# Retention by running sums of weighted keys times values, in place of products of all pairs of tiles

## The chip, the cores and the metric

One Trainium2 chip, one of its cores. The metric is the device time of one launch in microseconds (us). The core's engines are named as in the profile: PE is TensorE (matrix multiplies and transposes), DVE is VectorE, ACT is ScalarE, POOL is GpSimd, SP is SyncE, which only issues transfers here. Each engine works through its own list of instructions in the order in which the program wrote them, and waits at an instruction until what that instruction reads is there.

## The reference, cut to what matters

The reference is a two-layer transformer on 512 image tokens and 256 context tokens, 1024 wide. Each layer is a mixer (projections of the normed tokens; then windowed attention, global attention and retention; then a gated merge) and a mixture-of-experts part. The change is in retention: 4 heads, keys of 128, values of 256, with a decay per head for each of two directions. For the image tokens, after the context states `s_f` and `s_b` have been summed up:

```
def step(state, qkv):                        # one chunk of 128 tokens
    s = einsum('bihd,bjhd->bhij', qc, kc) * decay_in
    o = einsum('bhij,bjhe->bihe', s, vc) + einsum('bihd,bhde->bihe', qc * q_decay, state)
    state = chunk_decay * state + einsum('bjhd,bjhe->bhde', kc * k_decay, vc)
...
o_f = retention_chunkwise(qr, kr, vr, lg_f, s_f, False)
o_b = retention_chunkwise(qr[:, ::-1], kr[:, ::-1], vr[:, ::-1], lg_b, s_b, True)[:, ::-1]
o_ret = retention_output(o_f + o_b, u_r)
```

In layer 0 the context tokens have a retention of their own (all pairs of context tiles); in layer 1 they have none. Everything is float32.

## The kernel before

A product of two float32 matrices is made of three fp32r matmuls: each operand is split into a high part (a cast on ACT) and a low part (a subtraction on DVE), and `mm3` multiplies high by high, high by low and low by high. `split` writes the two parts one after the other, ACT first, and DVE's subtraction reads what ACT has cast.

In each layer's mixer, `dense_gen` writes the projections: 18 blocks of columns (`AK`, `A0`, ..., `R0` to `R3` for retention, `U`, and the gates `Ga`, `Gs`, `Gr`), each for 6 token tiles of 128 (4 for some blocks in layer 1), each tile 24 matmuls of 512 columns. After every 3 of these matmuls it yields the nanoseconds they are reckoned at (650), and `drive` adds them up. When the sum passes a quantum, one step of the "side" work is written in between: a step of the attention generators, and after them a step of retention, `ret_gen`. The quantum is what is left of the projections divided by the weighted number of side steps left (`left`, `weight`), so that side work and projections end together. The side work is thus cut into steps, and between two steps of retention PE gets 6 or 9 matmuls of the projections. What a step asks of ACT and DVE has that much PE time to be done, since the next step's matmuls stand in PE's list right behind.

Retention of one head, before: a table `ds` of decays over all distances (GpSimd counts, DVE multiplies, ACT takes exponentials, two pieces of 704 columns); then three turns, each for a pair of token tiles (tiles 0 to 3 are image, 4 and 5 context): four loaded blocks of q and k are transposed on PE into the PSUM tile `rqkt`, and `split` makes high and low parts of q, k and of the values (`qT`, `kT`, `VH`, `VL`). Then, for each of the 6 key tiles, a score tile against all 4 query tiles (`rst`, 3 matmuls of 512 columns), a multiplication by decays (`rt`), a split (`rpH`, `rpL`), and one step later 12 matmuls of 256 columns into the output `ro`. In layer 0 the two context tiles follow, in the same manner with 256 columns. `finish` norms the output and stores it while the next head begins.

The buffers are rings: `hp` holds 13 tiles of 512 columns (loaded q, k, v, the split scores, and what the projections store), PSUM's `oac` holds two tiles (`rqkt`, `rst`).

Of the kernel before, what the change touches and what calls it, by code (L numbers as in the profile page):

```python
# [8 lines left out]
F32 = mybir.dt.float32  # L9
# [143 lines left out]
def tile_dit(ctx, tc, a, out):  # L153
# [451 lines left out]
    def mixer(l):  # L605
# [566 lines left out]
        def ret_gen():  # L1172
# [40 lines left out]
            fins = []  # L1213
            yield from need(*[("R0", m) for m in range(6)])
            ld(0, 0)
            ld(0, 1)
            for h in range(4):
                blk = f"R{h}"

                ds = kv.tile([128, 1408], F32, tag="kv", name=f"rds{l}{h}")  # L1220
                di = pp.tile([128, 704], F32, tag="P", name="rdi")
                d2 = pp.tile([128, 704], F32, tag="P", name="rd2")
                for i in range(2):
                    sl = ds[:, i * 704:(i + 1) * 704]
                    nc.gpsimd.iota(di, pattern=[[1, 704]], base=-640 + i * 704, channel_multiplier=-1,
                                   allow_small_or_imprecise_dtypes=True)
                    nc.vector.tensor_scalar(d2, di, 0.0, lg[:, h:h + 1], op0=OP.max, op1=OP.mult)
                    nc.vector.tensor_scalar(di, di, 0.0, nlgb[:, 4 + h:5 + h], op0=OP.min, op1=OP.mult)
                    nc.vector.tensor_tensor(d2, di, d2, op=OP.add)
                    nc.scalar.activation(sl, d2, AF.Exp)  # L1230
                    yield 100
# [4 lines left out]
                for m in range(0, 6, 2):  # L1236
                    has_q = m < NIMG or ctx_q
                    if m + 2 < 6:
                        ld(h, m + 2)
                        ld(h, m + 3)  # L1240
                    ps = oac_tile("rqkt")
                    pv = ps.rearrange("p (m c t) -> p m c t", m=2, c=2)
                    vs = []
                    for i in range(2):
                        t = tl.pop((h, m + i))
                        if has_q:
                            nc.tensor.transpose(pv[:, i, 0, :], t[:, 0:128], ident)
                        nc.tensor.transpose(pv[:, i, 1, :], t[:, 128:256], ident)
                        vs.append(t[:, 256:512])
                    c = slice(m * 128, (m + 2) * 128)  # L1250
                    for j, T in ((0, qT), (1, kT)):
                        if j == 0 and not has_q:
                            continue
                        split(T[:, 0, c].rearrange("p (m t) -> p m t", m=2),
                              T[:, 1, c].rearrange("p (m t) -> p m t", m=2), pv[:, :, j, :])
# [3 lines left out]
                dctx = ot.tile([128, 2, 512], F32, tag="ot", name="rdctx")  # L1259
                for lt in range(2):  # L1260
                    cf = 256 - 128 * lt + 640
                    cb = -512 - 128 * lt + 640
                    nc.gpsimd.tensor_tensor(dctx[:, lt, :], ds[:, cf:cf + 512], ds[:, cb:cb + 512], op=OP.add)
                for grp in range(2 if ctx_q else 1):
                    qts = list(range(NIMG)) if grp == 0 else [4, 5]
                    nt = len(qts)
                    w = nt * 128
                    q0 = qts[0] * 128
                    kts = list(range(6)) if grp == 0 else [4, 5]
# [3 lines left out]
                    for ki, kt in enumerate(kts + [None]):  # L1273
                        if (grp == 1 or not ctx_q) and h < 3 and ki == max(len(kts) - RLD, 0):
                            yield from need(*[(f"R{h + 1}", m) for m in range(6)])
                            ld(h + 1, 0)
                            ld(h + 1, 1)
                        nxt = None
                        if kt is not None:
                            ps = oac_tile("rst")  # L1280
                            ks = slice(kt * 128, (kt + 1) * 128)
                            mm3(ps[:, 0:w], kT[:, 0, ks], kT[:, 1, ks], qT[:, 0, q0:q0 + w], qT[:, 1, q0:q0 + w],
                                True, True)
                            if grp == 0 and kt >= NIMG:
                                dd = dctx[:, kt - 4, :]
                            else:
                                c = 640 - 128 * (kt - qts[0])
                                dd = ds[:, c:c + w]
                            t = half("rt")
                            nc.vector.scalar_tensor_tensor(t[:, 0:w], ps[:, 0:w], ksc, dd, op0=OP.mult, op1=OP.mult)  # L1290
                            ph = half("rpH", F32R)
                            pl = half("rpL", F32R)
                            split(ph[:, 0:w], pl[:, 0:w], t[:, 0:w])
                            nxt = (ki, kt, ph, pl)
# [1145 lines left out]
```

## Time and profile before

| | us |
|---|---|
| time, median of 3 runs (lowest to highest) | 2956.02 (2948.24 to 2957.04) |
| the profiled execution: its own time | 2947.53 |
| its span, from the first to the last instruction | 2945.7 |
| PE busy in the span | 2778.4 (94%) |
| DVE busy | 1808.9 (61%) |
| ACT busy | 1281.2 (43%) |
| POOL busy | 362.3 (12%) |

An engine counts as busy while it has an instruction at work; matmuls are pipelined, so the time that a matmul costs is read from the start of one to the start of the next and not from its duration. Retention lies at 780 to 985 us (layer 0) and 2255 to 2420 us (layer 1).

### The profile page before, as it was taken

The numbers are of one execution on the slowest core, as the hardware profiler recorded it, in microseconds if no ns is written. First come the engines' busy times: TensorE is split into PE (matmuls) and PEld (weight loads), VectorE is DVE, ScalarE is ACT, GpSimd is POOL, SyncE is SP. The second block draws the span as 40 slices with busy tenths as digits, with TensorE's granted clock in tenths as the row PEclk, the third lists the DMA queues.
The fourth block names the chain that finished last, engine by engine and source line by source line (L and its number), as shares of the span: only waits on it lengthen the run. The fifth ranks groups of instructions, "written<-read, shape, count | busy, mean of one in ns | idle before, by whom it ended". The sixth has DMA issues, their size and how long they took to land. (4 is left out here: it accounts for less than half of the span.)

```text
span 2945.7 us, 42092 instructions
## 1 busy us (share of the span) xinstructions
PE 2778.4 (94%) x15259; PEld 2224.0 (75%) x15259; DVE 1808.9 (61%) x3222; ACT 1281.2 (43%) x2380; POOL 362.3 (12%) x427
## 2 busy tenths in 40 slices
PE   7999999999999999988999799999999999989986
PEld 4788888888887777776777478878988887767653
DVE  5676567667555456568676576667676655667432
ACT  4444445445444212227666454444455442216332
POOL 1220000000011000013322131100000100013211
PEclk8999999999999999998999999999999999989998
DMA  6333222223243577668999832222233447688998
GB/s 243 133 110 106 90 76 81 96 70 104 95 151 130 180 258 257 257 220 295 346 363 371 292 118 91 82 88 92 73 97 123 147 147 294 214 314 329 370 371 302
DMA packets 203925, 557.89 MB, mean 189 GB/s; under 512 B 27046, under 2 KB 51750, under 8 KB 203712
## 3 DMA queue, kind: packets, MB, share of 16 engines
q1 hardware_dynamic: 175840, 502.85, 47.6%
q0 software_dynamic: 10752, 25.03, 3.4%
q10 hardware_dynamic: 17120, 27.27, 2.5%
q8 instruction: 121, 1.98, 0.3%
q14 instruction: 92, 0.75, 0.1%
HBM read 462.22 MB, written 96.77 MB: 190 GB/s over the span
## 5 line engine op out<-in xcount | busy, mean ns | idle before, releaser
L114 DVE TENSOR_TENSOR wl<-raw,wh 128x1024 fp32r<-128x1024 f32 x474 | 565.2, 1220 | 148.9 <-ACT wh L102 144.6
L102 ACT CAST wh<-raw 128x1024 fp32r<-128x1024 f32 x474 | 484.7, 1050 | 351.9 <-DMA raw<-oT 131.4
L903 ACT ACTIVATE P<-sc,st 128x768 f32<-128x768 f32 (+4 forms) x240 | 176.2, 734 | 339.4 <-DVE st L901 211.0
L901 DVE TENSOR_REDUCE st<-sc 128x1 f32<-128x768 f32 (+4 forms) x240 | 178.5, 744 | 119.0 <-PE sc L179 113.3
L937 ACT CAST ptH<-pt 128x512 fp32r<-128x512 f32 x264 | 142.9, 591 | 125.1 <-PE pt L922 104.7
L179 PE MATMUL psb<-wl,wh 128*128 128x512 f32 x480 | 188.7, 393 | 7.1 <-DVE wl L114 7.1
L179 PE MATMUL psb<-wh,wh 128*128 128x512 f32 x480 | 191.7, 399 | 0.0
L179 PE MATMUL psb<-wh,wl 128*128 128x512 f32 x480 | 188.0, 392 | 2.2 <-DVE wl L114 2.2
L947 DVE TENSOR_TENSOR ptL<-pt,ptH 128x512 fp32r<-128x512 f32 x264 | 169.4, 681 | 9.2 <-ACT ptH L937 7.0
L922 PE MATMUL pt<-ident,P 128*128 128x128 f32 x1056 | 141.4, 275 | 13.8 <-ACT P L903 11.1
L922 PEld LDWEIGHTS pt<-ident,P 128*128 128x128 f32 x1056 | 119.7, 140 | 44.5 <-ACT P L903 30.2
L179 PE MATMUL psR<-wh,hH 128*128 128x512 f32 (+1 forms) x384 | 150.8, 393 | 0.0
L179 PE MATMUL psR<-wl,hH 128*128 128x512 f32 (+1 forms) x384 | 146.8, 382 | 2.7 <-DVE wl L114 2.7
L179 PE MATMUL psR<-wh,hL 128*128 128x512 f32 (+1 forms) x384 | 147.2, 383 | 0.0
L909 DVE TENSOR_SCALAR P<-P,st 128x768 f32<-128x768 f32 (+3 forms) x240 | 130.0, 542 | 8.5
L179 PEld LDWEIGHTS psb<-wh,wh 128*128 128x128 f32 x480 | 90.3, 188 | 45.3 <-issue 20.1
L495 POOL TENSOR_SCALAR rstd<-ss 128x4 f32<-128x4 f32 (+2 forms) x70 | 22.8, 326 | 825.8 <-ACT h L501 355.3
L179 PEld LDWEIGHTS psb<-wl,wh 128*128 128x128 f32 x480 | 90.5, 189 | 28.3 <-DVE wl L114 10.9
L179 PE MATMUL sc<-swkT,swqs 128*128 128x256 f32 x704 | 109.2, 281 | 2.2 <-ACT P L903 2.2
L179 PEld LDWEIGHTS psb<-wh,wl 128*128 128x128 f32 x480 | 90.5, 189 | 22.5 <-DVE wl L114 3.5
L179 PE MATMUL yps<-wh,hidT 128*128 128x512 f32 x320 | 105.6, 400 | 1.5 <-ACT wh L102 1.5
L1110 DVE COPY sc<-sink 128x1 f32<-128x1 f32 x160 | 25.7, 160 | 130.2 <-PE sc L179 123.1
(511 smaller groups left out, 6905.7 us busy)
## 6 DMA issues: line engine op xcount, KB each, us to landing
raw<-in_w_in_dram SPq DMA_DIRECT2D x136, 512.0 KB
raw<-in_w_gate_dram SPq DMA_DIRECT2D x128, 512.0 KB
raw<-in_w_up_dram SPq DMA_DIRECT2D x128, 512.0 KB
raw<-in_w_down_dram SPq DMA_DIRECT2D x128, 512.0 KB
raw<-in_w_mod_dram SPq DMA_DIRECT2D x96, 512.0 KB
raw<-in_w_br_dram SPq DMA_DIRECT2D x48, 512.0 KB
raw<-oT SPq DMA_DIRECT2D x30, 512.0 KB
raw<-in_w_out_dram SPq DMA_DIRECT2D x16, 512.0 KB
```

The lines of the kernel that those rows point to most:

```text
L102: self.nc.scalar.copy(c.h, c.raw)
L114: self.nc.vector.tensor_tensor(c.l, c.raw, c.h.bitcast(F32), op=OP.subtract)
L179: nc.tensor.matmul(ps, lhs, rhs, start=start, stop=stop, skip_group_check=share)
L495: nc.gpsimd.tensor_scalar(r[:, 0:cnt], ss, four / n, four * EPS, op0=OP.mult, op1=OP.add)
L901: nc.vector.reduce_max(st[:, 1, h:h + 1], s[:, 0:self.ns], axis=AX.X, negate=True)
L903: nc.scalar.activation(self.P[h][:, 0:self.ns], s[:, 0:self.ns], AF.Exp, bias=st[:, 1, h:h + 1], accum_out=st[:, 2, h:h + 1])
L909: nc.vector.tensor_scalar(self.P[h][:, 0:self.nk], self.P[h][:, 0:self.nk], st[:, 3, h:h + 1], None, op0=OP.mult)
L922: nc.tensor.transpose(pt[:, c * 256 + h * 128:c * 256 + (h + 1) * 128], self.P[2 * x + h][:, i * 128:(i + 1) * 128], ident)
L937: nc.scalar.copy(ph, src)
L947: nc.vector.tensor_tensor(pl, src, ph.bitcast(F32), op=OP.subtract)
L1110: nc.vector.tensor_copy(s[:, nk:nk + 1], sink[:, hd:hd + 1])
```

## The change

Retention of the image tokens no longer multiplies every key tile by every query tile. Four states, each a 128x256 matrix for either direction side by side (512 columns), are built one after the other: `state(0)` sums weighted context keys times values, `state(i)` multiplies the one before by a decay and adds the products of one key tile for each direction. `apply(i)` multiplies weighted queries by a state into the output. Scores are left only for each tile with itself (12 matmuls of 128 columns). The turns, now `turned(m)`, besides make the weighted queries (`rq`, split into `rQH`, `rQL`) and, from the loaded keys, keys weighted for both directions (`rk`, split into `rKH`, `rKL`). The context pair is turned first; in layer 1 it needs no transposes. The table of decays becomes 384 columns, two rows of 128 for the queries and six columns for the keys. A head has 12 steps in layer 0 (15 before) and 9 in layer 1 (12 before).

```diff
-                for m in range(0, 6, 2):
...
-                        nc.tensor.transpose(pv[:, i, 1, :], t[:, 128:256], ident)
...
-                    for i in range(2):
-                        split(VH[:, m + i, :], VL[:, m + i, :], vs[i])
-                    yield 300
...
-                    for ki, kt in enumerate(kts + [None]):
...
-                            mm3(ps[:, 0:w], kT[:, 0, ks], kT[:, 1, ks], qT[:, 0, q0:q0 + w], qT[:, 1, q0:q0 + w],
-                                True, True)
...
+                def turned(m):
...
+                        for j, T in ((0, qT), (1, kT)):
+                            split(T[:, 0, c].rearrange("p (m t) -> p m t", m=2),
+                                  T[:, 1, c].rearrange("p (m t) -> p m t", m=2), pv[:, :, j, :])
+                    if m < NIMG:
+                        q = half("rq")
+                        for x in range(2):
+                            nc.vector.scalar_tensor_tensor(
+                                q[:, x * 256:(x + 1) * 256].rearrange("p (m t) -> p m t", m=2), pv[:, :, 0, :], ksc,
+                                rw[:, x, :][:, None, :].to_broadcast([128, 2, 128]), op0=OP.mult, op1=OP.mult)
+                        QL[m] = half("rQL", F32R)
+                        split(QH[:, m // 2, :], QL[m], q)
+                    k = half("rk")
                     for i in range(2):
...
+                        for x in range(2):
+                            w = 3 * x + (m + i == (5 if x else 4))
+                            o = (2 * i + x) * 128
+                            nc.vector.tensor_scalar(k[:, o:o + 128], ts[i][:, 128:256], wk[:, w:w + 1], None,
+                                                    op0=OP.mult)
+                    KH[m], KL[m] = half("rKH", F32R), half("rKL", F32R)
+                    split(KH[m], KL[m], k)
                     for i in range(2):
...
+                        split(VH[:, m + i, :], VL[:, m + i, :], ts[i][:, 256:512])
+
+                def state(i):
+
+                    ps = oac_tile("rup")
+                    for x in range(2):
+                        kts = (4, 5) if i == 0 else (4 - i,) if x else (i - 1,)
+                        for kt in kts:
+                            m, j = kt - kt % 2, kt % 2
+                            ks = slice((2 * j + x) * 128, (2 * j + x + 1) * 128)
+                            for n, (k_, v_) in enumerate(((KH, VH), (KH, VL), (KL, VH))):
+                                mm(ps[:, x * 256:(x + 1) * 256], k_[m][:, ks], v_[:, kt, :],
+                                   kt == kts[0] and n == 0, kt == kts[-1] and n == 2, share=True)
...
+                    if i == 0:
+                        nc.scalar.copy(S[0][:, 0:512], ps)
+                    for x in range(2 if i else 0):
+                        c = slice(x * 256, (x + 1) * 256)
+                        nc.vector.scalar_tensor_tensor(S[0][:, c], old[:, c], wk[:, 3 * x + 2:3 * x + 3], ps[:, c],
+                                                       op0=OP.mult, op1=OP.add)
+                    split(S[1][:, 0:512], S[2][:, 0:512], S[0][:, 0:512])
+                    return S[1], S[2]
+
+                def apply(i, sh, sl):
+
+                    for x, t in ((0, i), (1, 3 - i)):
...
+                        for n, (q_, s_) in enumerate(((qh, sh), (qh, sl), (ql, sh))):
+                            mm(ov[:, t, :], q_, s_[:, c], False, i == 3 and n == 2, share=True)
...
+                fetch(h, 0)
+                turned(4)
+                yield 300
+                fetch(h, 2)
+                turned(0)
+                s0 = state(0)
+                yield 1500
+                turned(2)
+                yield 300
...
+                ph, pl = half("rpH", F32R), half("rpL", F32R)
+                split(ph, pl, t)
+                s1 = state(1)
+                yield 1500
...
+                apply(0, *s0)
+                s2 = state(2)
+                yield 1500
+                apply(1, *s1)
+                s3 = state(3)
+                yield 1500
...
+                apply(2, *s2)
+                yield 700
+                apply(3, *s3)
...
-        left = [5 * 2 * nq + 22, 5 * (4 * nq + 1), 4 * (15 if ctx_q else 12)]
+        left = [5 * 2 * nq + 22, 5 * (4 * nq + 1), 4 * (12 if ctx_q else 9)]
```

How the change moves instructions shows at three places of the first heads of layer 0. The first is PE's list where the last turn's parts are first used. Before, three score matmuls (`rst`) stand behind the projection's matmuls (`psGs`), and six more of those stand before the next three:

```order
L179 MATMUL psGs_4_8079<-wh_7858,hL_4_622 128x512
L179 MATMUL rst<-rqT_8052,rkT_8053 128x512 x3
L179 MATMUL psGs_4_8079<-wh_7858,hH_4_621 128x512
L179 MATMUL psGs_4_8079<-wl_7859,hH_4_621 128x512
L179 MATMUL psGs_4_8079<-wh_7858,hL_4_622 128x512
L179 MATMUL psGs_5_8151<-wh_7411,hH_5_689 128x512
L179 MATMUL psGs_5_8151<-wl_7412,hH_5_689 128x512
L179 MATMUL psGs_5_8151<-wh_7411,hL_5_690 128x512
L179 MATMUL rst<-rqT_8052,rkT_8053 128x512 x3
```

After, the transposes of `turned(2)` are followed by nine projection matmuls (the last three are shown), the 12 short scores and, with nothing in between, the six matmuls of `state(1)` (`rup`), the last three of which read the keys and values of tile 3:

```order
L179 MATMUL psGs_1_8202<-wh_8103,hH_1_406 128x512
L179 MATMUL psGs_1_8202<-wl_8104,hH_1_406 128x512
L179 MATMUL psGs_1_8202<-wh_8103,hL_1_407 128x512
L179 MATMUL rst<-rqT_8165,rkT_8166 128x128 x12
L179 MATMUL rup<-rVH_8167,rKH 128x256
L179 MATMUL rup<-rVL_8168,rKH 128x256
L179 MATMUL rup<-rVH_8167,rKL 128x256
L179 MATMUL rup<-rVH_8167,rKH 128x256
L179 MATMUL rup<-rVL_8168,rKH 128x256
L179 MATMUL rup<-rVH_8167,rKL 128x256
L179 MATMUL psGs_2_8342<-wh_7752,hH_2_475 128x512
```

So `state(1)` now stands one step behind the turn that makes what it reads. The second place is DVE's list of the same turns. Before, a turn is four subtractions (`rqT`, `rkT`, twice `rVL`), and after three turns come the scores:

```order
L188 TENSOR_TENSOR rqT_8052<-rqkt,rqT_8052 128x256
L188 TENSOR_TENSOR rkT_8053<-rqkt,rkT_8053 128x256
L188 TENSOR_TENSOR rVL_8055<-rqkv,rVH_8054 128x256 x2
L188 TENSOR_TENSOR rqT_8052<-rqkt,rqT_8052 128x256
L188 TENSOR_TENSOR rkT_8053<-rqkt,rkT_8053 128x256
L188 TENSOR_TENSOR rVL_8055<-rqkv,rVH_8054 128x256 x2
L1290 SCALAR_TENSOR_TENSOR rt<-rst,rds_8021 128x512
```

After, `turned(0)`, the split of the first state and the beginning of `turned(2)`:

```order
L188 TENSOR_TENSOR rqT_8165<-rqkt,rqT_8165 128x256
L188 TENSOR_TENSOR rkT_8166<-rqkt,rkT_8166 128x256
L1269 SCALAR_TENSOR_TENSOR rq<-rqkt,rds_8138 128x256 x2
L188 TENSOR_TENSOR rQL<-rq,rQH 128x512
L1279 TENSOR_SCALAR rk<-rqkv,rds_8138 128x128 x4
L188 TENSOR_TENSOR rKL<-rk,rKH 128x512
L188 TENSOR_TENSOR rVL_8168<-rqkv,rVH_8167 128x256 x2
L188 TENSOR_TENSOR rSL<-rS,rSH 128x512
L188 TENSOR_TENSOR rqT_8165<-rqkt,rqT_8165 128x256
L188 TENSOR_TENSOR rkT_8166<-rqkt,rkT_8166 128x256
```

The values' low parts, which `state` reads, moved from third and fourth in a turn to eleventh and twelfth, behind the weighted queries and keys. The third place is ACT's list between the two image turns of the second head: the cast of the first state, then the previous head's output (`roo`, with its store) and a cast of projection weights (`wh`), and only then the casts of the next turn:

```order
L1302 COPY rS<-rup 128x512
L187 CAST rSH<-rS 128x512
L1208 COPY roo<-rot 128x1024
L1209 DMA oT_109<-roo 128x4x256
L102 CAST wh_8686<-raw_8107 128x1024
L187 CAST rqT_8574<-rqkt 128x256
L187 CAST rkT_8575<-rqkt 128x256
L187 CAST rQH<-rq 128x512
L187 CAST rKH<-rk 128x512
```

What moved there: the state's copy and cast, and `rQH` and `rKH`, are new in ACT's list, so a turn has two more casts, each behind a result of DVE's.

## Rows read from the trace of the kernel before

**Rows 1.** The page, busy time of each engine (us, share of the span, instructions).
```profile
PE 2778.4 (94%) x15259; PEld 2224.0 (75%) x15259; DVE 1808.9 (61%) x3222; ACT 1281.2 (43%) x2380; POOL 362.3 (12%) x427
```

**Rows 2.** Busy time by stretch: us, PE, PEld, DVE, ACT, POOL, PEclk, DMA share, GB/s.
```profile
780.00:985.00 205.00, 200.16 (x1082) 170.20 (x1081) 102.50 (x178) 82.50 (x183) 24.53 (x31) 0.99 0.37 124
2255.00:2420.00 165.00, 164.48 (x892) 139.30 (x891) 95.52 (x155) 72.47 (x151) 19.77 (x23) 1.00 0.45 149
```

**Rows 3.** PE's timeline, one step of retention: start, us, what, count.
```profile
804.47 0.40 PE L179 MATMUL psGs<-wh,hH 128*128 128x512 f32 x1
...
806.54 0.84 PE L179 MATMUL rst<-rqT,rkT 128*128 128x512 f32 x3
807.22 0.28 PE L179 MATMUL ro<-rVH,rpH 128*128 128x256 f32 x1
...
808.65 0.40 PE L179 MATMUL psGs<-wh,hH 128*128 128x512 f32 x1
```

**Rows 4.** PE's timeline: a 128-column matmul of windowed attention.
```profile
605.21 0.22 PE L179 MATMUL sc<-maskr,identr 128*128 128x128 f32 x1
605.27 0.45 PE L179 MATMUL psU<-wh,hH 128*128 128x512 f32 x1
```

**Rows 5.** PE's timeline: the four transposes of a turn.
```profile
793.30 0.28 PE L1247 MATMUL rqkt<-ident,rqkv 128*128 128x128 f32 x1
...
793.66 0.47 PE L179 MATMUL psGs<-wh,hH 128*128 128x512 f32 x1
```

**Rows 6.** ACT's timeline, the same turn, and a split of scores.
```profile
793.94 0.37 ACT L187 CAST rqT<-rqkt 128x256 fp32r<-128x256 f32 x1 [0.35 <-PE rqkt L1248]
794.80 0.37 ACT L187 CAST rkT<-rqkt 128x256 fp32r<-128x256 f32 x1 [0.49 <-DVE rqT L188]
795.07 0.71 ACT L187 CAST rVH<-rqkv 128x256 fp32r<-128x256 f32 x2
...
801.77 0.62 ACT L187 CAST rpH<-rt 128x512 fp32r<-128x512 f32 x1 [1.38 <-DVE rt L1290]
```

**Rows 7.** DVE's timeline, the same turn, and the same split of scores.
```profile
794.35 0.42 DVE L188 TENSOR_TENSOR rqT<-rqkt,rqT 128x256 fp32r<-128x256 f32 x1 [1.58 <-ACT rqT L187]
795.21 0.42 DVE L188 TENSOR_TENSOR rkT<-rqkt,rkT 128x256 fp32r<-128x256 f32 x1 [0.44 <-ACT rkT L187]
...
800.16 0.75 DVE L188 TENSOR_TENSOR rVL<-rqkv,rVH 128x256 fp32r<-128x256 f32 x2
801.05 0.69 DVE L1290 SCALAR_TENSOR_TENSOR rt<-rst,rds 128x512 f32<-128x512 f32 x1
802.43 0.69 DVE L188 TENSOR_TENSOR rpL<-rt,rpH 128x512 fp32r<-128x512 f32 x1 [0.69 <-ACT rpH L187]
```

**Rows 8.** DVE's timeline: narrow operations elsewhere, and the scaling of a head's output.
```profile
169.96 1.12 DVE L801 SCALAR_TENSOR_TENSOR nA<-psA,rstd,gq 128x128 f32<-128x128 f32 x4
386.28 0.49 DVE L909 TENSOR_SCALAR P<-P,st 128x512 f32<-128x512 f32 x1
833.37 1.65 DVE L1199 SCALAR_TENSOR_TENSOR ron<-ro,rstd,rz 128x256 f32<-128x256 f32 x4
```

**Rows 9.** Costliest groups: weight splits of the projections (busy, mean ns, idle before).
```profile
L114 DVE TENSOR_TENSOR wl<-raw,wh 128x1024 fp32r<-128x1024 f32 x474 | 565.2, 1220 | 148.9 <-ACT wh L102 144.6
L102 ACT CAST wh<-raw 128x1024 fp32r<-128x1024 f32 x474 | 484.7, 1050 | 351.9 <-DMA raw<-oT 131.4
```

**Rows 10.** One tile's instructions: the stored output (count, ns min/median/max).
```profile
L1208 ACT COPY roo<-rot x12: 577/1010/1019, 841.5 to 2418.1; 128x1024 f32<-128x1024 f32 x8, 128x512 f32<-128x512 f32 x4
```

**Rows 11.** PE's timeline around its longest wait in retention.
```profile
938.25 0.33 PE L1247 MATMUL rqkt<-ident,rqkv 128*128 128x128 f32 x1 [3.42 <-DMA rqkv<-nat0R]
...
939.10 0.64 PE L179 MATMUL psGr<-wh,hH 128*128 128x512 f32 x1
...
942.10 0.63 PE L179 MATMUL psGr<-wl,hH 128*128 128x512 f32 x1
```

**Rows 12.** Busy time by stretch behind that wait (columns as in Rows 2).
```profile
940.00:942.00 2.00, 2.00 (x6) 1.61 (x5) 0.75 (x3) 1.26 (x2) 0.00 (x0) 0.50 0.19 69
```

More of the change, by code (lines that the diff above doesn't have):

```diff
@@ L1232, in ret_gen @@
+                nc.scalar.activation(strip, d2[:, 0:384], AF.Exp)
+                yield 100
                 qT = kv.tile([128, 2, 768], F32R, tag="kv", name=f"rqT{l}{h}")
@@ L1259, in ret_gen @@
[L1259 to L1269, printed above, removed]
+                QH = ot.tile([128, 2, 512], F32R, tag="ot", name="rQH")
@@ new lines, in apply, with next_head @@
+                def apply(i, sh, sl):
+                    for x, t in ((0, i), (1, 3 - i)):
+                        qs = slice(x * 256 + t % 2 * 128, x * 256 + t % 2 * 128 + 128)
+                        qh, ql = QH[:, t // 2, qs], QL[t - t % 2][:, qs]
+                        c = slice(x * 256, (x + 1) * 256)
+                        for n, (q_, s_) in enumerate(((qh, sh), (qh, sl), (ql, sh))):
+                            mm(ov[:, t, :], q_, s_[:, c], False, i == 3 and n == 2, share=True)
+                def next_head():
+                    if h < 3:
+                        yield from need(*[(f"R{h + 1}", m) for m in range(6)])
+                        fetch(h + 1, 4)
@@ new lines, in ret_gen @@
+                fetch(h, 0)
[7 more added lines that the diff above has]
+                yield 300
+                ps = oac_tile("rst")
+                for t in range(NIMG):
+                    c = slice(t * 128, (t + 1) * 128)
+                    for n, (k, q) in enumerate(((0, 0), (0, 1), (1, 0))):
+                        mm(ps[:, c], kT[:, k, c], qT[:, q, c], n == 0, n == 2, share=True)
@@ new lines, in ret_gen @@
+                yield 1500
+                o = att_tile("ro")
+                ov = o.rearrange("p (i d) -> p i d", i=4)
+                for i in range(NIMG):
+                    c = slice(i * 128, (i + 1) * 128)
+                    for n, (p_, v_) in enumerate(((ph, VH), (ph, VL), (pl, VH))):
+                        mm(ov[:, i, :], p_[:, c], v_[:, i, :], i % 2 == 0 and n == 0, False, share=True)
+                apply(0, *s0)
+                s2 = state(2)
+                yield 1500
+                apply(1, *s1)
@@ L1270, in ret_gen @@
+                s3 = state(3)
+                yield 1500
+                if not ctx_q:
+                    yield from next_head()
+                apply(2, *s2)
+                yield 700
+                apply(3, *s3)
+                fins.append(1)
+                side.append(finish(h, list(range(NIMG)), o))
+                yield 100
+                if ctx_q:
                     o = att_tile("ro")
@@ L1272, in ret_gen @@
                     pend = None
-                    for ki, kt in enumerate(kts + [None]):
[L1274 to L1277, printed above, removed]
+                    for kt in (4, 5, None):
+                        if kt == 4:
+                            yield from next_head()
                         nxt = None
@@ L1289, in ret_gen @@
-                            t = half("rt")
[L1290 to L1294, printed above, removed]
+                            c = 128 - 128 * (kt - 4)
+                            t = half("rt")
+                            nc.vector.scalar_tensor_tensor(t[:, 0:256], ps[:, 0:256], ksc, strip[:, c:c + 256],
+                                                           op0=OP.mult, op1=OP.mult)
@@ L1306, in ret_gen @@
                     fins.append(1)
-                    side.append(finish(h, qts, o))
+                    side.append(finish(h, [4, 5], o))
                     yield 100
@@ L2023 @@
 TURN = [(1, 4), (1, 5), (1, 6)]
-RLD = 2
 MCAP = 3
```

84 lines of the change are left out of this document (46 added, 38 removed).

## The prediction

> **What bounds the kernel now.** I read the page's busy times first: PE is busy for 2778.4 of 2945.7 us, no other engine for more than 61% [rows 1]. Then the stretches of retention: in layer 0 PE is busy 200.2 of 205 us, in layer 1 164.5 of 165, while DVE is busy 50 and 58% of them and ACT 40 and 44% [rows 2]. So PE sets the pace there. A matmul taken out is worth its spacing in PE's list, and every wait at a matmul is paid in full, because the projections' matmuls stand behind it in the same list. That DVE and ACT have room on average doesn't say that they have it within one step.
>
> **What PE saves.** Prices are start to start. Nine projection matmuls take 2.07 us, 0.23 each; three scores of 512 columns 0.68; twelve output matmuls of 256 columns 1.43, 0.12 each [rows 3]. A matmul of 128 columns takes 0.06 [rows 4]. Four transposes take 0.36 [rows 5]. Taken out per head: 18 scores of 512 (4.1 us) and 72 output matmuls (8.6), 12.7 us. Put in: 30 matmuls for the states, 24 that apply them and 12 within tiles, 66 of 256 columns (7.9 us), and 12 scores of 128 (0.7), 8.6 us. That is 4.1 us less in each of four heads; layer 1 also loses the two key transposes of the context pair, 4.3 us. Layer 0's context part stays. In all 34 us. Should the 128-column scores cost as much as 256 (0.12), 6 us of it would go.
>
> **What the turns cost.** Here is the other side. In a turn ACT and DVE hand the same data back and forth. From rows: ACT's cast of q to DVE's subtraction 0.41 us (793.94 to 794.35), from there to ACT's next cast 0.45, again 0.41 to DVE, then 0.34 for DVE to get on [rows 6, 7]: at 1.6 us q and k are split. Today two subtractions of values follow, 0.33 apart (0.75 for two of 0.42) [rows 7], and the turn is done in 2.3 us, about what one step gives PE to do.
>
> After the change, a turn of image tiles goes on like this, as DVE's list has it. Two weighted queries from PSUM: 0.39 each, the spacing of the four 256-column operations that took 1.65 us [rows 8]; to ACT, cast of 512 columns, back to DVE: 0.5 and 0.66 (801.77 to 802.43) [rows 6, 7]; low part 0.61: now 3.8 us. Four key products of 128 columns: at most 0.26 each (1.12 us for four of 0.34, from PSUM), at least 0.12 (a quarter of the 512-column scaling in 0.49) [rows 8]; I take 0.26, whose width is the same: 4.8. To ACT 0.1, cast 0.66, low part 0.61: 6.2. Two low parts of values: 6.9 us. The values that `state` wants come last, three times later than today.
>
> Between the two image turns DVE also has the first state's low part, which waits for ACT's copy and cast (0.6 each, as wide as `rpH` [rows 6]). With time 0 at the first cast of `turned(0)`: DVE has done that turn at 6.9, ACT the state's cast at 7.2, DVE its low part at 7.9. The second turn's first subtraction starts there, so its clock runs from 7.5: keys are split at 9.1, the values of tile 3 at 14.4.
>
> PE on the same clock, by rows 3 to 5, in a head of layer 1 with nine projection matmuls between steps: `state(0)` ends at 1.15, nine matmuls 3.2, transposes 3.6, nine matmuls 5.65, six scores 6.0. The next scores need the keys split at 9.1: a wait of 3.1 us. Then scores and the first half of `state(1)` until 9.9; its second half needs the low values of tile 3: a wait of 4.5 us, until 14.4. So **7.6 us of waits** in a head that has none now, against 4.3 saved. After that the list eases: `apply` reads states made a step earlier.
>
> In layer 0 `turned(4)` has a part in it too. Its chain (splits 1.6, keys 1.1, cast 0.66, low parts 0.61 and 0.67) takes 4.7 us, and PE reaches `state(0)` at about 2.2: with eight matmuls left behind the last value, 2 us of waits, and 9.2 in the head.
>
> Later heads have more in the way. In layer 0, ACT's list puts a weight cast (1.05 us [rows 9]) or a gate, and the output of the head before (1.0 [rows 10]), between the two turns: 2 us more; and the scaling of the last output stands ahead of `rt`, so that the next output matmuls wait some 0.7. That makes 11.9 in each of three heads. In layer 1, two heads have six projection matmuls in place of nine once (0.7 less cover), three have the 1.65 us scaling before `rt` (about 1.1 paid), and the third has two weight splits of 1.2 between the turns and one behind them: about 39 us for the four. Sum: 9.5 (with a gate in the first head) + 36 + 39 = **84 us**. From below: key products at 0.12 take off 11 us, and with nothing in later heads but the clean chain it would be 56. From above: 3.4 us more per head if a load or a buffer comes late, 111.
>
> **The clock.** The one long wait in retention today, 3.42 us for a load, was followed by matmuls 0.43 us apart in place of 0.23 for some 3 us [rows 11], with a granted clock of 0.50, which is 1.2 GHz [rows 12]: 1.6 us for eight matmuls. The new second wait is longer than that. I take 6 us in all, between 0 and 13 (eight heads at 1.6), since part of the slow time falls where PE then waits for `rpL` anyway.
>
> The Trainium skill (TensorE: Matmul & The Clock Gate, section "HAM oscillation — how this bites in real kernels") says that a loop which lets TensorE stand in each round finds its clock at half speed each time, and that this comes on top of the wait. By that rule all eight heads pay and the sum is 7 us higher. By the row alone one wait of this size did so, and this trace has no other in retention.
>
> **The rest.** The decay tables shrink on GpSimd, DVE and ACT; PE waits for none of these three there (0.5 us of idle in all of layer 1's stretch [rows 2]), and they stand a step ahead of the turn that reads them, so I count nothing; if they came late, the turn would start later by at most one such step. The loads are as many and still one step ahead. With 12 and 9 steps per head the quantum grows by 4 and 6% (weighted steps 290 to 278 and 221 to 209), so attention is spread a little wider; its matmuls and the projections' are the same, and I count nothing. `rt` and `rpL` (six times per head, now once) leave DVE with a total about 2 us larger per head; its 42 to 50% of free time hides that outside the turns.
>
> **Sum.** 84 of waits, 34 saved, 6 of clock: +56 us on the execution's own 2947.5, 1.8 us more than its span: 3003.5. That execution is 8.5 us under the median of the three runs and within their spread; I don't add the difference. About 0.3% (9 us) is what a measurement of this kernel can tell from no change.
>
> **The rivals.** First, *faster*: the turns keep up, and the 34 us remain in part. The place is DVE's list in `turned`; the point from which it decides is a wait of 4.25 us per head, that is, values of tile 3 at 11 us and not at 14.4, each turn in 5.2. For it speaks that DVE waits for ACT during a third of a turn in my chain, and that I took the dearer price for the keys. Against it, the alternation is in the lists and its rows are of this very stretch. Without any wait it would be 2913 us; I put it at 2925. Second, *about even*: only the clean chain is paid, with cheap keys, and attention gains by its wider spacing: waits of 40 to 55 us, 2953 to 2968. Third, *worse*: the ring `hp`. Queries and keys of a head now stay in 8 of its 13 buffers while projections store from the rest, so a load, or a cast on ACT, waits for a store. Each would add about what the late load cost, 3.4 us [rows 11]; in every head, with the clock, that is 111 + 13 - 34, 3038 us and more. It speaks for it that such a wait is there today, against it that only one head has it. Last, *the change doesn't do what it says*: PE isn't relieved because 128-column scores are bound by their weight loads. The row of the short matmul [rows 4] speaks against it; at 0.12 it costs 6 us and changes nothing else.
>
> **Chances.** My forecast, 2970 to 3035 us: 0.66. Faster rival 0.12; even 0.12, half of it within 0.3% of no change; worse 0.10. So faster 0.12, same 0.06, slower 0.82. The range reaches into the even rival and a little into the worse one: 2955 to 3045.
>
> **What would show it.** In the new profile PE is idle some 10 us per head where it now has next to none, with waits of `rup` and `rst` for `rVL` and `rkT` on DVE, longest about 4 us; scores start to start at 0.06; a granted clock of 0.5 behind the waits. DVE shows `rVL` of tile 3 14 us after the first cast of `turned(0)`. I am wrong if `rup` finds its operands ready, if keys cost well under 0.26 us, or if DVE and ACT overlap where I have them alternate.

## The result, and the profile after

The changed kernel takes 3019.91 us (median of 4 runs, 3015.40 to 3023.89), the kernel before 2952.61 (4 runs beside it): 1.0227 times as long, 95% interval 1.0200 to 1.0255. The profiled execution takes 3015.4 us with a span of 3013.6, 67.9 more than the span of before. So it is slower, 67 us where 56 were forecast.

The page's busy times, which answer to [rows 1]:

```profile
PE 2785.0 (92%) x15155; PEld 2228.3 (74%) x15155; DVE 1831.2 (61%) x3362; ACT 1303.5 (43%) x2440; POOL 342.0 (11%) x451
```

PE runs 104 matmuls fewer and is yet busy 6.6 us longer, and idle for 228.6 us in place of 167.3. DVE and ACT hardly have more to do. The stretches of retention, by stretch as in [rows 2] (they lie later here, and hold less projection work):

```profile
800.00:1025.00 225.00, 192.45 (x985) 160.99 (x984) 118.57 (x255) 97.99 (x219) 12.33 (x37) 0.91 0.35 119
2285.00:2480.00 195.00, 165.77 (x837) 139.20 (x836) 109.57 (x238) 86.30 (x190) 8.89 (x36) 0.86 0.36 119
```

PE, which had next to no idle time there, now stands for 32.6 of 225 us and 29.2 of 195, and its granted clock falls from 0.99 and 1.00 to 0.91 and 0.86: part of the time it stands at the lower of its two levels, 1.2 GHz in place of 2.4. What it waits for, in the waits of layer 0's stretch and then of layer 1's (waiter, releaser, us in total, times, longest):

```profile
PE rup L179 <- ACT rVH L187: 13.5, 7, 2.7
PE rst L179 <- ACT rkT L187: 9.3, 4, 3.3
PE rqkt L1262 <- DMA rqkv<-nat0R: 4.7, 1, 4.7
PE rup L179 <- DVE rVL L188: 2.3, 8, 0.4
...
PE rqkt L1262 <- DMA rqkv<-nat1R: 11.1, 4, 6.4
PE rup L179 <- ACT rVH L187: 10.4, 5, 2.7
PE rst L179 <- ACT rkT L187: 3.9, 3, 1.6
```

States (`rup`) wait for values and scores (`rst`) for keys, both products of the turns: with the smaller waits of these two kinds that are left out here, 42.4 us in both layers. Loads take 15.8 us besides. One later head of layer 0 in PE's timeline (start, us, what, count, idle time before):

```profile
867.43 0.60 PE L1262 MATMUL rqkt<-ident,rqkv 128*128 128x128 f32 x4
869.03 0.38 PE L179 MATMUL rup<-rVH,rKH 128*128 128x256 f32 x1 [1.00 <-ACT rVH L187]
869.79 0.39 PE L179 MATMUL rup<-rVL,rKH 128*128 128x256 f32 x1 [0.37 <-DVE rVL L188]
...
871.19 1.04 PE L1205 MATMUL rot<-ident,ron 128*128 128x128 f32 x8
...
875.74 0.40 PE L179 MATMUL psGr<-wh,hL 128*128 128x512 f32 x1
876.46 0.89 PE L179 MATMUL rst<-rqT,rkT 128*128 128x128 f32 x6 [0.32 <-ACT rS L1302]
880.65 1.58 PE L179 MATMUL rst<-rqT,rkT 128*128 128x128 f32 x6 [3.31 <-ACT rkT L187]
882.02 0.52 PE L179 MATMUL rup<-rVH,rKH 128*128 128x256 f32 x1
...
885.19 0.58 PE L179 MATMUL rup<-rVH,rKH 128*128 128x256 f32 x1 [2.22 <-ACT rVH L187]
885.98 0.58 PE L179 MATMUL rup<-rVL,rKH 128*128 128x256 f32 x1 [0.20 <-DVE rVL L188]
886.36 0.41 PE L179 MATMUL rup<-rVH,rKL 128*128 128x256 f32 x1
886.57 0.63 PE L179 MATMUL psGr<-wh,hH 128*128 128x512 f32 x1
...
889.83 0.39 PE L179 MATMUL psGr<-wh,hL 128*128 128x512 f32 x1
```

Read start to start, the head loses more than the idle times in brackets (7.4 us). From 875.97, when the last projection matmul is through, to 886.57 are 10.6 us, for twelve scores and six state matmuls that need 2.0: 8.6 lost. At the first state 3.4 us (867.79 to 871.19) go for 1.44 of work: 2.0 lost. Then eight `psGr` matmuls take 3.26 us (886.57 to 889.83) in place of 1.84: the granted clock is 0.50 from 879.4 to 889.6. Together 12.0 us. The same turns in DVE's timeline and in ACT's:

```profile
870.53 0.43 DVE L188 TENSOR_TENSOR rqT<-rqkt,rqT 128x256 fp32r<-128x256 f32 x1 [0.47 <-ACT rqT L187]
...
873.18 0.69 DVE L188 TENSOR_TENSOR rQL<-rq,rQH 128x512 fp32r<-128x512 f32 x1 [0.69 <-ACT rQH L187]
873.79 0.87 DVE L1279 TENSOR_SCALAR rk<-rqkv,rds 128x128 f32<-128x128 f32 x4
875.34 0.69 DVE L188 TENSOR_TENSOR rKL<-rk,rKH 128x512 fp32r<-128x512 f32 x1 [0.69 <-ACT rKH L187]
875.95 0.75 DVE L188 TENSOR_TENSOR rVL<-rqkv,rVH 128x256 fp32r<-128x256 f32 x2
877.09 0.69 DVE L188 TENSOR_TENSOR rSL<-rS,rSH 128x512 fp32r<-128x512 f32 x1 [0.38 <-ACT rSH L187]
...
885.17 0.75 DVE L188 TENSOR_TENSOR rVL<-rqkv,rVH 128x256 fp32r<-128x256 f32 x2
```

```profile
870.14 0.36 ACT L187 CAST rqT<-rqkt 128x256 fp32r<-128x256 f32 x1
...
876.96 1.01 ACT L1208 COPY roo<-rot 128x1024 f32<-128x1024 f32 x1
...
878.42 1.05 ACT L102 CAST wh<-raw 128x1024 fp32r<-128x1024 f32 x1 [0.45 <-ACT roo L1208]
879.37 0.36 ACT L187 CAST rqT<-rqkt 128x256 fp32r<-128x256 f32 x1
```

The first turn runs from 870.14 to 876.70, 6.56 us; the second starts at 879.37, behind the head's output and a weight cast; its last value is done at 885.92. ACT and DVE alternate: DVE is idle 0.69 us at each cast of 512 columns.

### The profile page after: what moved, and what is told of

Read it like the earlier page. It is cut to its first block, busy times and chain, and to the rows that moved or that the text cites. A ratio compares the mean times of both kernels' runs of the same rounds, so it can differ in the third digit from the quotient of the medians.

```text
span 3013.6 us, 42077 instructions
## 1 busy us (share of the span) xinstructions
PE 2785.0 (92%) x15155; PEld 2228.3 (74%) x15155; DVE 1831.2 (61%) x3362; ACT 1303.5 (43%) x2440; POOL 342.0 (11%) x451
## 5 line engine op out<-in xcount | busy, mean ns | idle before, releaser
L937 ACT CAST ptH<-pt 128x512 fp32r<-128x512 f32 x264 | 142.8, 591 | 137.8 <-PE pt L922 122.0
L922 PE MATMUL pt<-ident,P 128*128 128x128 f32 x1056 | 142.8, 276 | 18.6 <-ACT P L903 12.9
L179 PEld LDWEIGHTS psb<-wl,wh 128*128 128x128 f32 x480 | 90.8, 189 | 28.6 <-DVE wl L114 11.1
```

Source lines behind the costliest of these rows:

```text
L179: nc.tensor.matmul(ps, lhs, rhs, start=start, stop=stop, skip_group_check=share)
L922: nc.tensor.transpose(pt[:, c * 256 + h * 128:c * 256 + (h + 1) * 128], self.P[2 * x + h][:, i * 128:(i + 1) * 128], ident)
L937: nc.scalar.copy(ph, src)
```

## The experiments

Times are medians; each kernel ran beside the kernel before, and the ratio is to that. "Cover" is the PE work that stands in PE's list between a turn and the first matmul that needs it.

**More steps between the turns.** `yield 300` or `yield 1500` lets PE do one more step of projections.

```
                 turned(4)
                 yield 300
+                yield 300
...
                 s0 = state(0)
                 yield 1500
+                yield 1500
                 turned(2)
                 yield 300
+                yield 300
+                yield 300
...
-        left = [..., 4 * (12 if ctx_q else 9)]
+        left = [..., 4 * (16 if ctx_q else 13)]
```

> Four more steps per head (one behind the turn of tiles 4 and 5, one behind the first state, two behind the turn of tiles 2 and 3), and the planner's count of steps raised to 16 and 13. Each step gives PE some 2 us of projection work. Theory (a turn is a chain of ACT and DVE that is longer than its cover): of the 42 us that PE waits for turns under 10 are left, matmuls of 512 columns at half clock in retention fall from 75 to under 15, and the time is 2925 to 2955 us; the loads' 16 us may stay. Rival A (the 34 us of saved matmuls are not there): the waits go but the time stays at 2960 to 2985. Rival B (loads and buffers hold PE up, the turn only shows it): the waits change their names and the time stays over 2990.

2983.95 us, ratio 1.0107 (1.0090 to 1.0124): 36 us off the change, but 29 above the theory's range and inside that of rival A. The turns' waits did go (42.4 us in the change, 1.5 here, all in layer 0). But others remain: PE waits 10.5 us for `ron`, the scaled output, and 15.6 for loads, and 45 matmuls of 512 columns still run at half clock, where I had asked for under 15. Rival A is right in a small part: the scores, now without a wait, show their price, in PE's timeline and in that of the weight loads:

```profile
859.86 1.45 PE L179 MATMUL rst<-rqT,rkT 128*128 128x128 f32 x12
861.14 0.34 PE L179 MATMUL rup<-rVH,rKH 128*128 128x256 f32 x1
```

```profile
859.63 1.53 PEld L179 LDWEIGHTS rst<-rqT,rkT 128*128 128x128 f32 x12
861.08 0.19 PEld L179 LDWEIGHTS rup<-rVH,rKH 128*128 128x128 f32 x1
```

Twelve scores take 1.28 us, 0.107 each, and not the 0.06 of [rows 4]. Their weight loads (PEld, twelve in 1.45 us) keep the same pace: taken singly, scores and loads both start 0.11 us apart. So the change saves 3.5 us per head in layer 0 and not 4.1, 29 in all.

**Two steps only**, both behind `turned(2)`, and 14 and 11 in `left`.

> Two more steps per head, both behind the turn of tiles 2 and 3, ahead of the scores; the planner counts 14 and 11. Theory: 4 us more cover at the place of the two longest waits: the scores' wait for keys goes and that for the last values falls to under 1 us per head; the waits at the first state (some 1.4 us per head) and for loads stay. 2970 to 2988 us, above the kernel with four more steps by 20 to 45. Rival B: 3000 us or more.

3008.29 us, 1.0190 (1.0173 to 1.0207): 20 above the theory's range, and inside the rival's. The longest waits of layer 1's stretch, then DVE's timeline in layer 0 where its like stands:

```profile
PE rot L1205 <- DVE ron L1199: 21.1, 3, 7.4
PE psGs L179 <- DVE wl L114: 7.0, 2, 4.3
```

```profile
908.59 0.43 DVE L188 TENSOR_TENSOR rqT<-rqkt,rqT 128x256 fp32r<-128x256 f32 x1 [1.04 <-ACT rqT L187]
...
914.00 0.75 DVE L188 TENSOR_TENSOR rVL<-rqkv,rVH 128x256 fp32r<-128x256 f32 x2
914.67 0.87 DVE L1199 SCALAR_TENSOR_TENSOR ron<-ro,rstd,rz 128x256 f32<-128x256 f32 x2
```

`finish` counts its pauses in steps, while turns take time. With two steps put in, the transposes of the head before come up while DVE is still in the second turn, and `ron` stands behind all of it. The waits for keys are gone, and those for values are down from 27.4 to 8.6 us; but 41 us of waits for `ron` over both layers took their place.

**Weighted queries left out**: no `rq`, `rQH`, `rQL`; `apply` reads `qT`.

```
-                        qh, ql = QH[:, t // 2, qs], QL[t - t % 2][:, qs]
+                        qh, ql = qT[:, 0, qs], qT[:, 1, qs]
```

> The weighted queries are left out: no products of queries by their tables, no cast and no low part of them; the states are applied to the unweighted high and low parts of the queries, so that the output lacks that weighting. PE's list stays as it is. Theory: by the durations after the change (0.75 for the two products, 0.62 the cast, 0.6 the low part, and the handoffs) each turn of image tiles is some 2.1 us shorter, the second one ends 4.2 us earlier, and of the waits for keys and values 20 to 30 us go, with part of the slow clock: 2980 to 2998 us. Rival B (loads and buffers): 3005 us or more.

3041.51 us, 1.0303 (1.0285 to 1.0322), slower than the change. But it leaves out part of the result, so that other tokens go to other experts, and layer 0's expert stage runs matmuls that the other kernels don't have (one tile's instructions in that stage):

```profile
L179 PE MATMUL g<-w,xH x16: 390/564/797, 1686.6 to 1696.9; 128*128 128x512 f32 x16
```

Between the same two matmuls at its ends that stage takes 442 us, and 382 in the change. So I read it by stretch: up to the end of retention layer 0 is 19 us shorter than the change (995.9 against 1015.2), and layer 1, from its first projection to its output projection, 17 us (775.1 against 792.0). These 36 us lie in the 22 to 40 that the theory's range asked for, and the waits for keys and values fall from 42.4 to 18.7 us while those for loads stay. The whole time says nothing of it.

**Loads one step earlier.**

```
             fetch(0, 4)
+            fetch(0, 0)
...
                         fetch(h + 1, 4)
+                        fetch(h + 1, 0)
...
-                fetch(h, 0)
+                fetch(h, 2)
                 turned(4)
                 yield 300
-                fetch(h, 2)
                 turned(0)
```

> The loads of tiles 0 and 1 of the next head are issued with those of tiles 4 and 5, and tiles 2 and 3 a step earlier too: two more buffers of the ring are held. Theory: only the 15.8 us that PE waits for loads can go, with some slow clock behind them: 2998 to 3010 us, and the waits for keys and values stay at 38 to 48 us. Rival B: without late loads the turns start earlier and keep up, 2985 us or less. If the ring of buffers is too small for it, DVE or ACT waits for buffers and it is 3015 us or more.

3016.46 us, 1.0223 (1.0206 to 1.0240), not to be told from the change, and above the theory's range. PE's waits for loads fall in layer 1 from 11.1 to 2.0 us, but 4.0 for a weight (0.6 in the change) and 2.3 more for values come in their place. In the change those loads come late because SP issues them in order behind weight loads that wait for a buffer (SP's timeline of the change, layer 1):

```profile
2355.05 5.28 SPq L83 DMA_DIRECT2D raw<-in_w_in_dram  x2
2360.38 2.11 SPq L1180 DMA_DIRECT2D rqkv<-nat1R  x4
```

**The turns' work alone, in the kernel before**: the products, casts and low parts of keys are made in each turn, those of queries in the two image turns, and no matmul reads them; all matmuls stay, no states.

```
                     for j, T in ((0, qT), (1, kT)):
...
+                    if m < NIMG:
+                        q = half("rq")
...
+                        split(half("rQH", F32R), half("rQL", F32R), q)
+                    k = half("rk")
...
+                    split(half("rKH", F32R), half("rKL", F32R), k)
```

> The kernel before, all its matmuls, with the work of the new turns alone added to its turns: two products of queries, four of keys, their casts and low parts, whose results nothing reads. No states and no strip of decay; loads as before. Theory (the turn's chain is longer than a step): PE now waits at the first scores for the second turn's queries and keys, 2 to 5 us in each of eight heads and more where a weight cast or an output stands between: 2970 to 2995 us. Rival (ACT and DVE have the room, the loss comes from what PE reads in the changed kernel or from its loads): 2950 to 2962 us.

3033.20 us, 1.0286 (1.0267 to 1.0306): 81 us more, where the theory had 18 to 43: beyond its range, and far from the rival's. Waits of layer 0's stretch:

```profile
PE rst L179 <- DVE rq L1260: 14.2, 4, 5.3
PE rot L1205 <- DVE ron L1199: 9.4, 3, 3.6
```

The scores read no `rq`. Their wait is for the PSUM tile: `oac` holds two, and DVE reads `rq` out of the second turn's `rqkt` before a score may be written there. So this wait is not at the place where the change has its own, but it is for the same thing, the progress of ACT and DVE in the turns. Loads don't explain it: PE waits 3.8 us for them in both layers, 3.6 in the kernel before. So the loss is there without a state, with the old matmuls, and comes from what the turns put on ACT and DVE.

**Transposes of the output two steps later**, on top of the four steps: `pause(4)` in place of `pause(2)` in `finish`.

> The kernel with four more steps per head, and the transposes of a head's scaled output two steps later (five steps in place of three stay as they are, the second pause is four in place of two). With the four steps the waits for turns had gone, and the transposes waited 10.5 us for the scaled output on DVE in their place. Theory (turn work fills DVE, so that what stands behind it in DVE's list comes late): these waits go with what they cost around them, 2966 to 2976 us, the loads' 16 us stay. Rival (PE finds another wait, since DVE or ACT is the bound of this stretch): 2980 us or more.

2975.09 us, 1.0089 (1.0071 to 1.0107), as the theory said: no wait for `ron` is left in retention, and those for loads stay at 15.2 us.

**Loads earlier too**, as above and for the first head a step ahead.

> As the kernel with four more steps and later transposes, and the loads of a head's tiles one step earlier, the first head's a step ahead of its turn. Theory: the waits of PE for loads fall from 16 to under 4 us and no other wait takes their place, now that the turns have cover: 2945 to 2960 us. Of 29 us saved in matmuls (the 128-column scores cost 0.107 us each, not 0.06) no more than a third is then seen, the rest is lost to slow clock, restarts and the attention stretch of layer 1. Rival (the earlier loads only move the wait to weights, as they did alone): 2965 us or more.

2980.66 us, 1.0106 (1.0089 to 1.0123): missed, and in the rival's range. In retention PE waits for loads for 1.6 us in place of 15.2, and layer 1's retention is 7 us shorter. But other waits do take their place: those of the states for values grow from 8.7 to 14.0 us, and 44 matmuls of 512 columns run at half clock in place of 25. The attention ahead of layer 1's retention is 7.5 us longer too (618.2 and 610.7), with waits of `pt` for the softmax's `P` of 16.9 us in place of 9.6. The profiled execution (2972.93 us) is the shortest of the four and as long as that of the kernel without this edit (2973.61), so the trace doesn't show the 6 us that the medians differ by.

**Keys on GpSimd and one more step**: `nc.gpsimd.tensor_scalar` for `k`, `yield 1500` ahead of `ro`, 17 and 14 steps.

> As the kernel before it in this set, with the products of keys on GpSimd in place of DVE and one more step ahead of the output matmuls. Theory (DVE's list in a turn sets the end): each turn is some 0.8 us shorter on DVE and the waits for rpH go: 2938 to 2955 us, if GpSimd takes under 0.6 us for a product of 128 columns. Rival: GpSimd is slower than that, or slows DVE while both run, and the keys come late at the states: 2960 us or more.

2959.69 us, 1.0035 (1.0022 to 1.0048), 5 above the theory's range. The costliest group of GpSimd:

```profile
L1281 POOL TENSOR_SCALAR rk<-rqkv,rds 128x128 f32<-128x128 f32 x96 | 71.2, 759 | 63.2 <-DMA rqkv<-nat0R 28.8 <-ACT rds L1239 26.7 <-PE rup L179 6.5
```

A product of keys takes 0.76 us on average (0.60 in the median, at most 1.69), longer than the theory asked, and waits of the states for values stay at 12.5 us. Still it is 21 us less than without the two edits; which of them gave it isn't shown.

**Values first, queries last, and two steps out again** (those behind `state(0)` and one behind `turned(2)`; 15 and 12, as many as before the change). Keys stay on GpSimd, at the head of the turn:

```
                     ts = [tl.pop((h, m + i)) for i in range(2)]
+                    k = half("rk")
...
+                    for i in range(2):
+                        split(VH[:, m + i, :], VL[:, m + i, :], ts[i][:, 256:512])
...
-                        QL[m] = half("rQL", F32R)
-                        split(QH[:, m // 2, :], QL[m], q)
...
                     split(KH[m], KL[m], k)
-                    for i in range(2):
-                        split(VH[:, m + i, :], VL[:, m + i, :], ts[i][:, 256:512])
+                    if m < NIMG:
+                        QL[m] = half("rQL", F32R)
+                        split(QH[:, m // 2, :], QL[m], q)
```

> As the kernel with keys on GpSimd, and in a turn the values are split first, and the cast and low part of the weighted queries come last, so that what the next state reads is ready about 2 us earlier. Two of the five added steps per head are taken out again, so that layers have 15 and 12 steps per head, as many as the kernel before the change. Theory (with the turn shorter, three more steps are cover enough, and each step taken out gives the softmax of attention its projections back, whose waits for P had grown from 5 to 13 us in layer 1): 2938 to 2955 us. Rival (it is the turn's total work, not its order, that PE waits for): the waits for values or keys come back and it is 2960 us or more.

**2930.10 us**, 0.9923 (0.9909 to 0.9938): below the theory's range, and 22.5 us faster than the kernel before. It has the edits to steps, transposes, loads and keys in it besides. Its stretches of retention:

```profile
794.00:968.00 174.00, 170.91 (x976) 147.92 (x975) 101.32 (x196) 89.43 (x207) 44.56 (x85) 1.00 0.38 129
2265.00:2408.00 143.00, 141.54 (x792) 121.98 (x791) 90.22 (x163) 79.52 (x166) 34.79 (x70) 1.00 0.46 152
```

PE is idle 4.5 us of both, at full clock, and no matmul of 512 columns is slow there (75 in the change).

**One step less**, that behind `turned(4)`.

> As that kernel with one step per head less again, the one behind the turn of tiles 4 and 5: 14 and 11. Theory: the first state now waits for GpSimd's keys (four of 0.73 us, then cast and low part, some 4.5 us after the load's turn, against 2.1 us of cover), 2 us in each of eight heads, against a gain of 3 to 5 us in attention: 2945 to 2970 us, above the kernel with one step more by 5 to 15. Rival (attention's cover is worth more): below it.

2959.26 us, 1.0023 (1.0011 to 1.0034): inside the theory's range, but 29 above the kernel with the step, more than the 5 to 15 I gave. The waits of layer 1:

```profile
PE rup L179 <- ACT rKH L187: 6.5, 4, 4.0
PE psGs L179 <- DVE wl L114: 6.1, 2, 3.4
```

**The old order in the turn**, all else as in the fastest kernel.

> The fastest kernel so far with the order of the turn put back: weighted queries, keys and values in the order of the change; keys stay on GpSimd, 15 and 12 steps, loads and transposes as there. Theory (the order in the turn sets when the states find their values): waits for values come back at the states, 1 to 3 us a head with the clock behind them: 2945 to 2965 us. Rival (the two steps taken out again, and not the order, gave the gain over the kernel with 17 and 14 steps): 2927 to 2936 us.

2952.92 us, 1.0002 (0.9990 to 1.0014): the order in the turn alone is worth 23 us, and without it the edited kernel is even with the kernel before. The order moves keys and values ahead and the queries' parts to the end; which of these moves counts isn't shown. Waits of layer 1:

```profile
PE rup L179 <- ACT rVH L187: 4.4, 4, 1.1
PE rup L179 <- DVE rVL L188: 1.9, 4, 0.5
```

**Keys back on DVE**, all else as in the fastest kernel.

> The fastest kernel so far with the products of keys back on DVE, first in the turn. Theory (work on DVE's list in a turn delays all behind it): the splits of queries, keys and values start 0.85 us later in each of three turns, and waits of under 1 us come back at the scores and states: 2933 to 2948 us. Rival (GpSimd's 0.73 us a product is the slower way, so that the keys come earlier from DVE and nothing is lost): 2925 to 2932 us.

2933.83 us, 0.9936 (0.9920 to 0.9953): its interval overlaps that of the fastest, so GpSimd's part in the gain isn't settled, and small.

## Why the prediction was right, and where a size was off

**The direction and the cause held; that the sum came so near is in part luck.** The work of the turns, put alone into the kernel before, cost 81 us. Cover and order in the turns took the waits away, and then 22.5 of the 29 us saved in matmuls came out.

**The turn's chain.** 6.9 us forecast, 6.56 measured; four key products take 0.87 us of it, where the chain had 1.04. With the output and a weight cast between the turns I put the second one's start at 9.5 and tile 3's values at 16.4 us behind the first cast; they are at 9.2 and 15.8. In the clean chain it was 14.4, and so it is in the first head of layer 1 (ACT's first cast, DVE's last low parts, 2337.14):

```profile
2322.77 0.37 ACT L187 CAST rqT<-rqkt 128x256 fp32r<-128x256 f32 x1 [0.77 <-PE rqkt L1262]
2336.39 0.75 DVE L188 TENSOR_TENSOR rVL<-rqkv,rVH 128x256 fp32r<-128x256 f32 x2
```

A later head of layer 0 was to lose 11.9 us and 0.75 of clock; the head above lost 12.0, clock included. Part of this is no idle time in the profile: it is in the spacing of matmuls behind a wait and at half clock. The waits carry the name of ACT's cast, since in ACT's list the values stand behind the cast of the keys; I had named DVE's low part, which comes 0.2 to 0.4 us later.

**The sum over retention.** From the first transposes to the first matmul of the output projection the two layers take 197.4 and 172.8 us. Their matmuls by full-clock spacings (0.23, 0.12, 0.107 a score, 0.09 a transpose) make 149.5 and 122.0, so 47.9 and 50.8 are lost. In the kernel before it is 9.8 and 3.6 (some matmul records are missing in both). So **85 us** more are lost, where the sum had 90, and 29 stand against them. Idle time is 48 of the 85.

**The clock: 21 us in place of 6.** The same stretches, with the granted clock behind the busy times:

```profile
817.77:1015.20 197.43, 170.90 (x892) 144.55 (x892) 103.76 (x238) 83.34 (x197) 12.33 (x37) 0.90 0.31 102
2321.27:2494.10 172.83, 145.54 (x718) 121.98 (x719) 96.33 (x208) 75.38 (x164) 8.37 (x29) 0.84 0.34 112
```

The granted clock is at its lower level for 41 and 55 us of them, 3.4 in the kernel before. Where another wait follows, slow matmuls cost nothing of their own: the wait ends when ACT or DVE is done, however soon PE comes to it. Those behind the last wait of each slow stretch take 22.7 us above their full-clock spacings, 1.4 in the kernel before: 21 more, where I took 6 and allowed 13 at most. My 13 counted matmuls of 512 columns alone (75 ran at half clock, 8 before); those of 128 and 256 pay too. Behind the second turn's wait the clock was at half in all eight heads, with six to nine matmuls of 512 columns each. The Trainium skill (TensorE: Matmul & The Clock Gate, "HAM oscillation — how this bites in real kernels") says this of a loop with a wait in each round, and by it the sum would have been 7 us higher; the trace agrees on how often, and the cost is higher.

**The waits: 64 us in place of 84.** That is what is left of the 85, with 9 us for loads in it. The turns were hardly quicker than forecast. In the first head of layer 1 it was PE that came later: behind a wait for a load its clock was at half (2323.2 to 2326.6), it was through with the first six scores 7.4 us behind the first cast and not 6.0, and its wait for keys was 1.6 us and not 3.1. How the rest of the 20 us divides over the heads is not worked out. So two terms were off by 20 and by 15 us, one each way, and the sum by 5.

**Other terms that were mis-sized.** "A matmul of 128 columns takes 0.06" was the wrong row for a score: at 0.107, 5 of the 34 us were never there. That is what the last rival said, by 0.12 and 6 us. "The loads are as many and still one step ahead", counted at nothing: PE waits 15.8 us for them, 11.1 in layer 1, through SP's list. Yet earlier loads alone gave nothing, and nothing again on top of more steps, so this is no 16 us that could be had back. "Attention is spread a little wider; I count nothing": outside the stretches above 12 us were lost (67.9 - 85 + 29). Of these 6.6 are the first heads' waits for loads, 4.7 and 1.9 us, which end where these stretches begin, and 4 lie between layer 1's retention and its merge, where 12 matmuls ran at half clock; that leaves some 1 us for the wider attention.

**The rivals.** *Faster* asked for turns of 5.2 us; they took 6.56. A kernel in which PE hardly waits in retention does come near it, 2930 us against 2925, but only with values ahead of the queries, three more steps and the edits to loads and transposes. *Worse* named the ring `hp`: in layer 1 SP does stand 18.6 and 17.6 us at loads of a next head until DVE's `rKL` frees a buffer, but the weight loads that come next in its list then wait 14 and 19 us for DVE's `wl`, so no loss by the ring is shown.

**What I had wrong in the experiments** is that cover can be added step by step. Steps also count the pauses of `finish`, so two of them brought 41 us of waits for the output, and one step taken from the fastest kernel cost 29.

## What to carry to other kernels

Where an in-order PE has no idle time, matmuls that are saved pay only if what feeds the others keeps up: lay the new operand's chain over ACT and DVE on a clock, handoffs included, beside the cover that PE's list gives it, and look at the loss start to start, since idle time was only 48 of 85 us here. Price the clock behind a wait that comes back in each round, for all matmuls there and not the widest alone. Order a chain by who needs its results first: the same operations with keys and values ahead of the queries' parts were worth 23 us. When a kernel paces side work by steps, each step added or removed also moves every other wait that is counted in steps.

## What was not expected of the hardware

A run of 128-column matmuls with new weights each goes at 0.107 us, at the pace of the weight loads beside it, and so costs nearly what 256 columns cost (0.12). A wait also costs PE some 0.3 us behind it that no view calls idle: at full clock, the matmul at 869.03 is followed by the next 0.76 us later, of which 0.37 are a wait and 0.12 its own, so 0.27 are left. At 885.19 it is 0.79, with a wait of 0.20; there the clock is 0.50 and its own spacing 0.22, which leaves 0.37. Scaling 128 x 128 values took GpSimd 0.60 us in the median, with single ones up to 1.69, and DVE 0.87 for four; though GpSimd is some three times slower at it, the kernel that has it there beside the splits was no slower than that with DVE (2930.1 and 2933.8 us).
